# Partial sums copied into the banks of the next products, in a new order of products

## The chip, the cores and the metric

The kernel runs on one core of a Trainium2 chip. The engines of the core work side by side and in order, each on its own list of instructions: TensorE (PE, matmuls, with its weight loads shown apart as PEld), VectorE (DVE), ScalarE (ACT), GpSimd (POOL) and SyncE (SP, which issues most DMAs; ACT issues some). PE writes only into PSUM, here eight banks of 128 x 512 fp32 values. The metric is the device time of one execution in microseconds, the median over several.

## The reference

One layer of a hybrid encoder over 2048 prompt tokens and 64 sample tokens, 1024 wide, in fp32:

```python
mod = (c_act @ w_ada + b_ada)            # six modulation vectors
h = rmsnorm(x, g1) * (1 + sc1) + sh1
u, q, k, v, o, gates = split(h @ w_in)   # pooling mixer and mLSTM side by side
x = x + gt1 * (concat(pool_out, hs) @ w_out)
h2 = rmsnorm(x, g2) * (1 + sc2) + sh2
up = h2 @ w_up                           # 1024 -> 2 x 2816
conv = b_conv + sum(w_conv[j] * upp[:, j:j + T] for j in range(3))   # causal, width 3
a, g = split(conv)
x = x + gt2 * ((silu(g) * a) @ w_down)
y = rmsnorm(x, g_final)
```

It also returns the states that the next call needs (pooling rows, mLSTM matrices, the last two rows of up). The change lies in up = h2 @ w_up and what follows it; some small edits lie in the first stage and in the final norm.

## The kernel before, in words

**Precision.** Each fp32 operand is kept as two parts in PE's reduced fp32 format, hi (a rounded copy, made by ACT) and lo (what is left, made by DVE). A product of two such operands is three passes: hi x hi, hi x lo and lo x hi (PASSES, lines 401 and 1441). Weights come from memory as raw tiles and are split in work_out (L359 on ACT, L362 on DVE). Some splits are kept in memory for later groups (wsplit) and then loaded whole.

**Stages.** Up to about 800 us the kernel does the attention side, in four groups of 512 tokens. Its first stage makes the modulation vectors and the v projection in one (first, L969): for each quarter of the 1024 inputs it builds two slices of h (hi on ACT, lo on DVE) and multiplies them with slices of the weights. From there on it does the feed-forward part, in three groups of 704 tokens (fgroups; g is the group, o the group's record), each in four parts of 5, 5, 6 and 6 pairs (PARTS). A pair f stands for 128 columns of a and the 128 columns of g that gate them. A part first makes its pairs (class Pair, products) and then multiplies them with their rows of w_down for all eight blocks of 128 output columns (down, L1707), adding into x3 (down_end, L1722).

**A pair.** The up-projection uses a Strassen-Winograd scheme with seven half-size products instead of eight: the tokens of the group are two halves of 352, the 1024 inputs two halves of 512. For each pair PE makes seven products, each 12 matmuls of 128 x 352 (L1441), named after their operand on the token side: B11, B21, T2, T3, B22, T1 and T4. Their weights are up_unit 0 (B11), 1 (B21), 3 (T4) and the sums WS2 (T2), WS3 (T3), WS4 (B22) and WS1 (T1), made once by the kernel. Three PSUM banks take them: b1 holds B11, then B11 + T2, then B11 + T2 + T1; b2, which is also b4, holds B21 and then, newly begun, B22; b3 holds T3 and then T3 + T4. The results are

```
a, first half:  B21 + s1     (s1 = B11, copied by ACT, L1480; sum on DVE, L1493)
g, first half:  b3 + u2      (u2 = B11 + T2, L1489; sum_g0, L1449)
a, second half: B22 + u4     (u4 = B11 + T2 + T1, L1504; sum_a, L1449)
g, second half: T3 + u4      (sum_g1, L1449)
```

They are written to ea and eg, from which scale_a and scale_g (ACT, L1424), taps_a and taps_g (DVE, L1429, two each), silu (ACT, L1535), gate (DVE), split_hi (ACT) and split_lo (DVE) make the split operand of the down-projection. The tiles s1, u2, u4 and ea have one buffer each.

**The order.** In the feed-forward stage the order on PE, ACT, DVE and POOL is that in which the Python code calls them (manual_schedule); the order of SP's DMAs is left to a scheduler, apart from DMAs marked keep_in_program_order. The steps of three pairs are interleaved by hand in products: those of this pair, of the one before (old) and of the one before that (older). T4 of the pair before is done by old.last_product, between products of this pair; at the first pair of a part old is None. Weight units are fetched by pump, called ahead of each product, in the order of the list stream: up to seven units ahead, with six tiles for split weights and four for raw ones, and the splits of the next four are issued to ACT and DVE by the same call. Banks come in turn from two pools (mm_ps), six of them here.

**Background work.** Generators in bg are advanced by one step at a time (tick) between products: prepare (norm and token-side operands of the next group, which ACT stores to Bd), reload (which loads them, in the order of BN), final (final norm of the group before, stored by SP, L1606) and final_end (the same for the last group). x3 is loaded from x2d by load_x2 (L1576), two slices per pair.

Of the kernel before, what the change touches and what calls it, by code (L numbers as in the profile page):

```python
# [12 lines left out]
ALU = mybir.AluOpType  # L13
# [32 lines left out]
BN = ("B11", "B21", "T2", "T3", "B22", "T1", "T4")  # L46
# [13 lines left out]
def tile_layer(ctx: ExitStack, tc: tile.TileContext, xT, vecs, cst, rst, rowv, w_mod, w_ada, w_qkou, w_v, w_pool,  # L60
# [242 lines left out]
    for g in range(NFG):  # L303
        for (f0, f1_) in PARTS:
            late = []
            for f in range(f0, f1_):
                stream += [(up_unit(f, 0), 512), (up_unit(f, 1), 512)] + late
                stream += [sum_unit(g, f, i) for i in (WS2, WS3, WS4, WS1)]
                late = [(up_unit(f, 3), 512)]
# [91 lines left out]
    PASSES = ((0, 0), (0, 1), (1, 0))  # L401

# [386 lines left out]
    if True:  # L789
# [128 lines left out]
        def first():  # L918
# [44 lines left out]
            def cells(qn, us):  # L963
                for hv, to in ((1, ps), (0, ps2)):
                    w, n = us[1 - hv].w, VC[hv]
                    for k in (2 * qn, 2 * qn + 1):
                        for ti in range(4):
                            for pi, (a, b) in enumerate(PASSES):
                                pe.matmul(to[ti][:, :n], h[k][:, b, ti * P:(ti + 1) * P],  # L969
                                          w[:, a, k % 2 * n:(k % 2 + 1) * n],  # L970
                                          start=(hv == 1 and k == 0 and pi == 0), stop=(k == KD - 1 and pi == 2),
                                          skip_group_check=hv == 0)
                            yield
# [480 lines left out]
    class Pair:  # L1454
# [9 lines left out]
        def products(self, old):  # L1464
# [15 lines left out]
            act.activation(self.s1, b1[:, :FH], AF.Copy)  # L1480
# [9 lines left out]
            rest((old, Pair.scale_g))  # L1490
            self.ea = ext_tile(o, f, "a")
            for (a, b, d) in spans(o, 0):
                dve.tensor_tensor(out=self.ea[:, d:d + b - a], in0=b2[:, a:b], in1=self.s1[:, a:b], op=ALU.add)  # L1493
            self.b3 = mm_ps()
            product(self.b3, Bo, "T3", True)
            rest((old, Pair.taps_g))
            tick(1)
            product(self.b4, Bo, "B22", True)
            rest((old, Pair.silu))
            product(b1, Bo, "T1", False)  # L1500

        def copy_u4(self):
            self.u4 = half_tile("u4")
            act.activation(self.u4, self.b1[:, :FH], AF.Copy)  # L1504

        def sum_a(self):
            plus(self.o, 1, self.ea, self.u4, self.b4)
# [81 lines left out]
    def final(o, x3, ssum):  # L1589
# [13 lines left out]
        for k in range(KD):  # L1603
            dve.scalar_tensor_tensor(out=x3[k], in0=x3[k], scalar=V[:, V_GF + k:V_GF + k + 1], in1=box[0],
                                     op0=ALU.mult, op1=ALU.mult)
            nc.sync.dma_start(out=yT[k, :, o.t0:o.t0 + FT], in_=x3[k])  # L1606
# [3 lines left out]
    def final_end(o, x3, sums, lo, hi):  # L1610
# [7 lines left out]
        dg = fscr()  # L1618
# [5 lines left out]
        nf, rem = w // P, w % P  # L1624
        blks = [(0, nf, P), (nf, nf + 1, rem)] if rem else [(0, nf, P)]
        for (a, b, n) in blks:
            v = dg[:n, a * P:a * P + (b - a) * n].rearrange("p (t c) -> p t c", c=n)
            dve.tensor_tensor(out=v, in0=ident[:n, :n].unsqueeze(1).broadcast_to([n, b - a, n]),
                              in1=rs[:n, a:b].unsqueeze(2).broadcast_to([n, b - a, n]), op=ALU.mult)
        for _ in range(4 if lo == 0 else 0):  # L1630
            yield
        pb = m2_ps()
        for (a, b, n) in blks:
            c = slice(a * P, a * P + (b - a) * n)
            pe.matmul(pb[:, c], ones[:n, :], dg[:n, c], start=True, stop=True)
# [220 lines left out]
```

## Time and profile before

| | |
|---|---|
| three runs | 2226.63, 2229.96, 2235.10 us; median 2229.96 |
| profiled execution | 2230.7 us; its span 2228.9 us, mean granted PE clock 0.994 |
| PE | busy 2193.3 us, 98% of the span |
| DVE, ACT, POOL | 1573.4, 1004.7 and 197.5 us (71%, 45%, 9%) |
| up-projection matmuls (L1441) | 5544, busy 887.5 us |
| down-projection matmuls (L1707) | 3168, busy 508.2 us |
| DMA | 493.52 MB, mean 221 GB/s |

Times are in microseconds from the span's start unless marked ns. PE's busy time is not time at its peak, since matmuls are pipelined and their ends modelled. A row of the timeline has start, duration, engine, line, operation, out<-in, shape and count, and in brackets the idle time before it with what ended it. A row of the table by line has busy time, mean ns of one, and the idle time before the group with what ended most of it. A row of the table of waits has the waiting engine and line, what it waited for, us in total, times, and the longest. A row of a window has its length, the busy time of PE, PEld, DVE, ACT and POOL with instructions, the granted PE clock, the DMA engines' share and GB/s.

### The profile page before, as it was taken

The page shows a single profiled execution, that of the slowest core. Times are in us where ns is not written, and L with a number is a line of the kernel's source. Part 1 is how long each engine was busy: PE and PEld are TensorE (multiplying, and loading weights), DVE is VectorE, ACT ScalarE, POOL GpSimd, SP SyncE. Part 2 cuts the span into 40 slices and gives each one's busy share as a digit, 9 for nine tenths or more (in the row PEclk, how much of TensorE's full clock was granted, in tenths as well). Part 3 has the DMA queues.
Part 4 walks back from the last instruction along what each step waited for, and adds up shares of the span by engine and source line. Part 5 has one row for each costly group of instructions (what it writes and reads, how often), then busy time and mean ns, then how long its engine had stood idle before and what let it go on. Part 6 is the DMA issues. An engine that isn't in the chain of part 4 may idle for free.

```text
span 2228.9 us, 37979 instructions
## 1 busy us (share of the span) xinstructions
PE 2193.3 (98%) x13720; PEld 2080.2 (93%) x13720; DVE 1573.4 (71%) x2909; ACT 1004.7 (45%) x1992; POOL 197.5 (9%) x475
## 2 busy tenths in 40 slices
PE   7999999999999989999999999999999999999998
PEld 6888888878899989999999999999999999999997
DVE  4878568577856678687868677677757685757474
ACT  3554335234334446464636444445435353445254
POOL 0010001001000100010000110000001210101012
PEclk9999999999999999999999999999999999999999
DMA  9967996997899466657656874556458654353442
GB/s 335 343 237 250 330 313 213 321 314 245 281 309 306 143 234 224 205 180 250 220 160 213 295 251 156 196 191 218 145 170 266 199 196 160 111 179 120 144 152 80
DMA packets 276445, 493.52 MB, mean 221 GB/s; under 512 B 24953, under 2 KB 103417, under 8 KB 276257
## 3 DMA queue, kind: packets, MB, share of 16 engines
q1 hardware_dynamic: 266784, 468.77, 63.1%
q10 hardware_dynamic: 9472, 22.32, 2.6%
q8 instruction: 108, 1.77, 0.3%
q14 instruction: 81, 0.66, 0.1%
HBM read 382.77 MB, written 108.22 MB: 220 GB/s over the span
## 4 chain that ended last, share of the span: by engine, by line
PE 60%; DMA 1%; DVE 1%; issue 0%; ACT 0%; POOL 0%; POOLq 0%; SPq 0%; ACTq 0%; DVEq 0%
PE mm L1441 37%; PE mm L1707 22%; DMA wt<-wsum 1%; DMA yT<-x 0%; ACT tg L1424 0%; DVE tg L1429 0%; DMA wt<-wsplit 0%; DMA x<-x2d 0%; ACT wt L359 0%; PE m L1595 0%; DVE ta L1429 0%; ACT ta L1424 0%; PE m L1621 0%; DVE hx L722 0%; DVE wt L362 0%
## 5 line engine op out<-in xcount | busy, mean ns | idle before, releaser
L1441 PE MATMUL mm<-hx,wt 128*128 128x352 f32 x5544 | 887.5, 321 | 8.8 <-DVE wt L362 5.0
L1441 PEld LDWEIGHTS mm<-hx,wt 128*128 128x128 f32 x5544 | 881.7, 188 | 10.3 <-DVE wt L362 5.2
L1707 PE MATMUL mm<-av,wt 128*128 128x352 f32 (+2 forms) x3168 | 508.2, 321 | 0.0
L1707 PEld LDWEIGHTS mm<-av,wt 128*128 128x128 f32 x3168 | 502.7, 188 | 1.8 <-DVE x L1722 0.4
L415 PE MATMUL mm<-hl,wt 128*128 128x512 f32 (+2 forms) x1920 | 397.4, 359 | 3.7 <-DMA wt<-hl_kept 2.8
L362 DVE TENSOR_TENSOR wt<-raw,wt 128x512 fp32r<-128x512 f32 (+3 forms) x494 | 307.2, 638 | 88.5 <-ACT wt L359 78.7
L415 PEld LDWEIGHTS mm<-hl,wt 128*128 128x128 f32 x1920 | 313.0, 188 | 52.4 <-issue 7.6
L359 ACT ACTIVATE wt<-raw 128x512 fp32r<-128x512 f32 (+3 forms) x494 | 271.2, 570 | 191.3 <-PE mm L1707 81.6
L415 PE MATMUL mm<-mx,wt 128*128 128x512 f32 (+1 forms) x960 | 186.0, 353 | 2.2 <-DVE wt L362 1.6
L1722 DVE SCALAR_TENSOR_TENSOR x<-mm,MOD,x 128x352 f32<-128x352 f32 (+4 forms) x224 | 106.6, 527 | 114.0 <-PE mm L1707 113.9
L415 PEld LDWEIGHTS mm<-mx,wt 128*128 128x128 f32 x960 | 158.7, 188 | 27.6 <-DVE wt L362 1.9
L1429 DVE SCALAR_TENSOR_TENSOR tg<-eg,V,tg 128x704 f32<-128x704 f32 (+1 forms) x132 | 125.7, 952 | 46.9 <-ACT tg L1424 44.4
L362 DVE TENSOR_TENSOR wt<-wt 128x512 fp32r<-128x512 f32 x176 | 121.9, 693 | 45.5 <-ACT wt L359 45.1
L359 ACT ACTIVATE wt<-wt 128x512 fp32r<-128x512 f32 x176 | 110.0, 626 | 69.9 <-DMA wt<-wsum 64.0
L1429 DVE SCALAR_TENSOR_TENSOR ta<-ea,V,ta 128x704 f32<-128x704 f32 (+1 forms) x132 | 125.7, 952 | 8.7 <-ACT ta L1424 6.3
L1564 DVE TENSOR_TENSOR av<-tg,av 128x704 fp32r<-128x704 f32 (+4 forms) x112 | 62.2, 589 | 46.7 <-ACT av L1556 46.4
L1535 ACT ACTIVATE tg<-tg 128x704 f32<-128x704 f32 (+1 forms) x66 | 52.4, 794 | 79.2 <-DVE tg L1429 79.2
L1489 ACT ACTIVATE u<-mm 128x352 f32<-128x352 f32 x66 | 30.6, 464 | 126.5 <-PE mm L1441 90.9
L1449 DVE TENSOR_TENSOR eg<-mm,u 128x352 f32<-128x352 f32 x154 | 70.2, 468 | 22.5 <-ACT u L1504 11.3
L196 DVE SCALAR_TENSOR_TENSOR acc<-raw,CA,acc 128x512 f32<-128x512 f32 x84 | 60.7, 746 | 30.3 <-DMA raw<-w_ada 30.3
L1480 ACT ACTIVATE s<-mm 128x352 f32<-128x352 f32 x66 | 30.6, 463 | 90.0 <-PE mm L1441 89.7
L1037 PE MATMUL mm<-wt,hl 128*128 128x256 f32 (+1 forms) x576 | 70.9, 282 | 0.0
(281 smaller groups left out, 1992.6 us busy)
## 6 DMA issues: line engine op xcount, KB each, us to landing
wt<-hl_kept SPq DMA_DIRECT2D x108, 512.0 KB, 5.7
raw<-w_up SPq DMA_DIRECT2D x198, 256.0 KB, 3.8
wt<-wsum SPq DMA_DIRECT2D x176, 256.0 KB, 4.0
wt<-wsplit SPq DMA_DIRECT2D x88, 512.0 KB, 4.3
raw<-w_down SPq DMA_DIRECT2D x96, 256.0 KB, 2.8
w<-w_up SPq DMA_DIRECT2D x88, 256.0 KB, 5.4
wsum<-w SPq DMA_DIRECT2D x44, 512.0 KB, 4.8
wsplit<-wt SPq DMA_DIRECT2D x44, 512.0 KB, 4.4
```

The costliest lines, as they stand in the source:

```text
L196: dve.scalar_tensor_tensor(out=acc[s], in0=w, scalar=CA[:, k, s:s + 1], in1=acc[s], op0=ALU.mult, op1=ALU.add)
L359: act.activation(u.w[:, 0, :u.n], u.raw[:, :u.n], AF.Copy)
L362: dve.tensor_tensor(out=u.w[:, 1, :u.n], in0=u.raw[:, :u.n], in1=u.w[:, 0, :u.n].bitcast(F32), op=ALU.subtract)
L415: pe.matmul(ps[bi][:, :hi - lo], U[:, a, k % 4 * P:(k % 4 + 1) * P], mv[k][:, b, lo:hi], start=(at == 0 and pi == 0), stop=(k == order[-1] ...
L1037: pe.matmul(ps[ti][:n, :cols], h[4 * kh + k4][:, b, lo:lo + n], U[:, a, k4 % 2 * cols:(k4 % 2 + 1) * cols], start=(kh == 0 and k4 == 0 and ...
L1429: dve.scalar_tensor_tensor(out=t[:, :E], in0=ext[:, j:j + E], scalar=wc(j, f), in1=t[:, :E], op0=ALU.mult, op1=ALU.add)
L1441: pe.matmul(ps[:, :FH], U[:, a, kc * P:(kc + 1) * P], Bo.at(nm, kc, b), start=(first and kc == 0 and pi == 0), stop=(kc == 3 and pi == 2), ...
L1449: dve.tensor_tensor(out=ext[:, d:d + b - a], in0=ps[:, a:b], in1=u[:, a:b], op=ALU.add)
L1535: act.activation(self.tg[:, :E], self.tg[:, :E], AF.Silu)
L1564: dve.tensor_tensor(out=cut(1), in0=self.of_tg(cut(0), a, b), in1=cut(0).bitcast(F32), op=ALU.subtract)
L1707: pe.matmul(ps[i][:, :hi - lo], U[:, a, k % 4 * P:(k % 4 + 1) * P], av[k](b, lo, hi), start=(k == 0 and (a, b) == PASSES[0]), stop=(k == n ...
L1722: dve.scalar_tensor_tensor(out=x3[n][:, a:b], in0=ps[i][:, a - lo:b - lo], scalar=gt2(n, s), in1=x3[n][:, a:b], op0=ALU.mult, op1=ALU.add)
```

## The change

The bank b2 now takes over what ACT and DVE added before. Once B11 is in b1, ACT copies b1 into b2, and B21 accumulates on that; ACT then copies the finished first half of a from b2 to ea (out_a). Once T1 is in b1, ACT copies b1 into b2 again and also to u4, B22 accumulates on the bank, and ACT copies the second half to ea at the start of the next pair (out_a1). The order of products in a pair becomes B11, (T4 of old), T2, B21, T1, T3, B22, and the stream of weights and BN follow it. In the first two pairs of all, one matmul prepares b2 for accumulation. sum_g0 stands ahead of taps_a, and sum_g1 follows T3 in its own pair. The step ahead of the down-projection follows suit.

The other edits: in the first stage the three passes of four matmuls each go in the order hi x hi, then lo weights, then lo of h, four tiles at a time; load_x2 in groups 1 and 2 loads three slices per pair, in program order; the output stores of final go to ACT's queue, one step behind their product; final_end broadcasts the statistics by matmuls with the identity as moving operand, without the DVE product of before, and takes fewer steps.

```diff
-BN = ("B11", "B21", "T2", "T3", "B22", "T1", "T4")
+BN = ("B11", "T2", "B21", "T1", "T3", "B22", "T4")
...
-                stream += [(up_unit(f, 0), 512), (up_unit(f, 1), 512)] + late
-                stream += [sum_unit(g, f, i) for i in (WS2, WS3, WS4, WS1)]
+                stream += [(up_unit(f, 0), 512)] + late + [sum_unit(g, f, WS2), (up_unit(f, 1), 512)]
+                stream += [sum_unit(g, f, i) for i in (WS1, WS3, WS4)]
...
     PASSES = ((0, 0), (0, 1), (1, 0))
+    HIGHS = ((0, 0), (1, 0), (0, 1))
...
-                        for ti in range(4):
-                            for pi, (a, b) in enumerate(PASSES):
-                                pe.matmul(to[ti][:, :n], h[k][:, b, ti * P:(ti + 1) * P],
...
-                            yield
+                        cell = [(pi, a, b, ti) for pi, (a, b) in enumerate(HIGHS) for ti in range(4)]
+                        for i, (pi, a, b, ti) in enumerate(cell):
+                            pe.matmul(to[ti][:, :n], h[k][:, b, ti * P:(ti + 1) * P],
...
+                            if i % 3 == 2:
+                                yield
...
-            rest((old, Pair.copy_u4), (older, Pair.gate))
+            rest((old, Pair.out_a1), (older, Pair.gate))
+            if o.g == 0 and f < 2:
+                pe.matmul(b2[:, :FH], ones_r, Bo.at("B11", 0, 0), start=True, stop=True)
             product(b1, Bo, "B11", True)
-            rest((old, Pair.sum_g1), (old, Pair.sum_a))
-            self.s1 = half_tile("s1")
-            act.activation(self.s1, b1[:, :FH], AF.Copy)
-            rest((older, Pair.split_hi))
-            product(b2, Bo, "B21", True)
-            rest((old, Pair.scale_a), (older, Pair.split_lo))
+            act.activation(b2[:, :FH], b1[:, :FH], AF.Copy)
+            rest((older, Pair.split_hi), (old, Pair.scale_a), (older, Pair.split_lo))
             if old:
                 old.last_product()
-            rest((old, Pair.taps_a), (old, Pair.sum_g0))
+            rest((old, Pair.sum_g0), (old, Pair.taps_a))
             product(b1, Bo, "T2", False)
             self.u2 = half_tile("u2")
             act.activation(self.u2, b1[:, :FH], AF.Copy)
             rest((old, Pair.scale_g))
+            product(b2, Bo, "B21", False)
             self.ea = ext_tile(o, f, "a")
-            for (a, b, d) in spans(o, 0):
-                dve.tensor_tensor(out=self.ea[:, d:d + b - a], in0=b2[:, a:b], in1=self.s1[:, a:b], op=ALU.add)
+            self.out_a(0)
+            product(b1, Bo, "T1", False)
+            act.activation(b2[:, :FH], b1[:, :FH], AF.Copy)
+            self.u4 = half_tile("u4")
+            act.activation(self.u4, b1[:, :FH], AF.Copy)
+            rest((old, Pair.taps_g))
             self.b3 = mm_ps()
             product(self.b3, Bo, "T3", True)
-            rest((old, Pair.taps_g))
             tick(1)
-            product(self.b4, Bo, "B22", True)
+            self.sum_g1()
             rest((old, Pair.silu))
-            product(b1, Bo, "T1", False)
-
-        def copy_u4(self):
...
-        def sum_a(self):
-            plus(self.o, 1, self.ea, self.u4, self.b4)
+            product(self.b4, Bo, "B22", False)
+
+        def out_a(self, half):
+            for (a, b, d) in spans(self.o, half):
+                act.activation(self.ea[:, d:d + b - a], self.b4[:, a:b], AF.Copy)
+
+        def out_a1(self):
+            self.out_a(1)
...
-            nc.sync.dma_start(out=x, in_=x2d[k, :, o.t0:o.t0 + FT])
+            got = nc.sync.dma_start(out=x, in_=x2d[k, :, o.t0:o.t0 + FT])
+            if o.g > 0:
+                tc.keep_in_program_order(got)
...
-            nc.sync.dma_start(out=yT[k, :, o.t0:o.t0 + FT], in_=x3[k])
+            yield
+            act.dma_start(out=yT[k, :, o.t0:o.t0 + FT], in_=x3[k])
...
-            v = dg[:n, a * P:a * P + (b - a) * n].rearrange("p (t c) -> p t c", c=n)
-            dve.tensor_tensor(out=v, in0=ident[:n, :n].unsqueeze(1).broadcast_to([n, b - a, n]),
-                              in1=rs[:n, a:b].unsqueeze(2).broadcast_to([n, b - a, n]), op=ALU.mult)
-        for _ in range(4 if lo == 0 else 0):
+        for _ in range(3 if lo == 0 else 0):
             yield
...
-            pe.matmul(pb[:, c], ones[:n, :], dg[:n, c], start=True, stop=True)
+        for ti, (t, n) in enumerate(tiles):
+            pe.matmul(pb[:, t - lo:t - lo + n], rs[:n, ti:ti + 1].broadcast_to([n, P]), ident[:n, :n],
+                      start=True, stop=True)
...
                     if lo == 0:
                         yield
-                        yield
...
-                    x3 += load_x2(o, range(len(x3), min(len(x3) + 2, KD)))
+                    x3 += load_x2(o, range(len(x3), min(len(x3) + (3 if o.g else 2), KD)))
...
-            pair.copy_u4()
-            todo.extend([both_of(pair.sum_g1, old.gate), both_of(pair.sum_a, old.split_hi), both_of(old.split_lo, pair.scale_a)])
+            pair.out_a1()
+            todo.extend([old.gate, old.split_hi, both_of(old.split_lo, pair.scale_a)])
```

More of the change, by code (lines that the diff above doesn't have):

```diff
@@ L966, in cells @@
                     for k in (2 * qn, 2 * qn + 1):
-                        for ti in range(4):
-                            for pi, (a, b) in enumerate(PASSES):
[L969 to L972, printed above, removed]
-                            yield
+                        cell = [(pi, a, b, ti) for pi, (a, b) in enumerate(HIGHS) for ti in range(4)]
+                        for i, (pi, a, b, ti) in enumerate(cell):
+                            pe.matmul(to[ti][:, :n], h[k][:, b, ti * P:(ti + 1) * P],
+                                      w[:, a, k % 2 * n:(k % 2 + 1) * n],
+                                      start=(hv == 1 and k == 0 and pi == 0), stop=(k == KD - 1 and pi == 2),
+                                      skip_group_check=hv == 0)
+                            if i % 3 == 2:
+                                yield
             for qn in range(4):
@@ L1617, in final_end @@
         rs = f1.tile([P, 5], F32, tag="rs", name="rs", bufs=2)
-        dg = fscr()
         for ti, (t, n) in enumerate(tiles):
```

7 lines of the change are left out of this document (removed).

## The prediction

> **What bounds the kernel now.** I read the page's busy times and chain first, then who TensorE (PE) waited for, then the timeline at the places that the change touches, then the rows by shape.
>
> ```profile
> span 2228.9 us, 37979 instructions
> PE 2193.3 (98%) x13720; PEld 2080.2 (93%) x13720; DVE 1573.4 (71%) x2909; ACT 1004.7 (45%) x1992; POOL 197.5 (9%) x475
> L1441 PE MATMUL mm<-hx,wt 128*128 128x352 f32 x5544 | 887.5, 321 | 8.8 <-DVE wt L362 5.0
> ...
> PE mm L1441 <- DVE wt L362: 5.0, 1, 5.0
> PE mm L969 <- DVE hl L913: 2.8, 4, 0.8
> PE mm L1441 <- ACT wt L359: 2.0, 2, 1.4
> PE mm L1441 <- DVE ea L1493: 1.8, 2, 1.3
> ```
>
> PE is idle for 2228.9 - 2193.3 = 35.6 us in all. In the up-projection (L1441), where most of the edit lies, it is idle for 8.8 us out of some 900, and five waits make up all of that. So work taken from VectorE (DVE) is not by itself time taken from the end: only PE's idle time can be won, and every new wait of PE is paid in full.
>
> **The change, part by part.** The profiled execution took 2230.7 us (1.8 around its span); the median of the runs is 2229.96, 0.7 lower. The sum is made against 2230.7.
>
> *Copies instead of sums.* Each of the 66 pairs loses two or three DVE sums into ea and a ScalarE (ACT) copy s, and gains two ACT copies from a bank into a bank and two or three from a bank into ea.
>
> ```profile
> L1480 ACT ACTIVATE s<-mm 128x352 f32<-128x352 f32 x66 | 30.6, 463 | 90.0 <-PE mm L1441 89.7
> L1493 DVE TENSOR_TENSOR ea<-mm,s 128x352 f32<-128x352 f32 x66 | 34.2, 519 | 1.1 <-PE mm L1441 1.0
> L1449 DVE TENSOR_TENSOR ea<-mm,u 128x352 f32<-128x352 f32 x44 | 22.7, 517 | 0.0
> ...
> 1636.70:1690.00 53.30, 53.30 (x338) 53.30 (x338) 40.19 (x60) 28.22 (x48) 3.91 (x16) 1.00 0.54 177
> ```
>
> The last row is four steady pairs (PE, PEld, DVE, ACT, POOL busy): PE is never idle, DVE has 40.2 and ACT 28.2 of 53.3 us. DVE loses 4 x 2 x 0.52 = 4.2 there and ACT gains 4 x 3 x 0.46 = 5.6, both under a full PE: worth nothing at the end and costing nothing, as long as no copy is late. The cover is what changes. Before, T2, which adds onto the bank that s is read from, came two products after B11. Now one product (T4 of the pair before) stands between, and B22, which adds onto the bank that the second copy fills, has one (T3). A product takes 12 x 0.158 = 1.9 us (53.30 / 338), and a copy needs 0.46: some 1.2 us to spare.
>
> *The first pair of each part.* Here old is None, so no T4 stands between: B11, copy, T2. Twelve times (3 groups x 4 parts) PE must wait. The timeline where the last part of group 1 begins, and the one place where T2 waited for s:
>
> ```profile
> 1625.29 9.03 PE L1441 MATMUL mm<-hx,wt 128*128 128x352 f32 x56
> 1627.39 0.47 ACT L1480 ACTIVATE s<-mm 128x352 f32<-128x352 f32 x1 [5.78 <-PE mm L1441]
> ...
> 1499.27 4.94 PE L1441 MATMUL mm<-hx,wt 128*128 128x352 f32 x29
> 1501.14 0.50 ACT L715 ACTIVATE fscr<-fscr 128x352 fp32r<-128x352 f32 x1 [2.27 <-DMA Bd<-fscr]
> 1502.64 0.44 ACT L1480 ACTIVATE s<-mm 128x352 f32<-128x352 f32 x1
> 1503.13 0.95 PEld L1441 LDWEIGHTS mm<-hx,wt 128*128 128x128 f32 x6 [0.18 <-ACT s L1480]
> ```
>
> The product after B11 would start at 1625.29 + 12 x 0.158 = 1627.19; the copy ends at 1627.86, and PE's weight load follows an end by 0.05 (1503.13 after 1502.64 + 0.44). That is 0.72 us, and a restart costs 0.09 more: in the row 1787.87 below, 7 matmuls after a wait take 1.36 us where 0.32 + 6 x 0.158 = 1.27 would do. 12 x 0.81 = 9.7 us. Bounds: the row has SBUF as its target, and no row shows ACT writing a bank; with no copy time at all 12 x 0.35 = 4.2, with the copy's time doubled, for a bank at both ends (0.93 us), 15.3. I take the row itself, the nearest. The Trainium skill (ScalarE: Activation LUTs, Step-by-step: what each stage is for) says that ScalarE writes PSUM faster than SBUF, and its page Perfetto Trace Analysis (Optimizing Scalar/DVE Operations) gives access overheads of about 51 ns against 93 ns. No run here shows it; by these figures the copy would be 0.42 us, an estimate, and the term 9.2 us.
>
> At one of the twelve (1499.27) ACT was late: B11 ended near 1501.33 and its copy began at 1502.64, behind splits that waited for a store. Between them two products hid it; now it is paid: 1.3 us (0 to 1.3). Another cost follows some waits: a slower pace.
>
> ```profile
> 1503.50:1510.50 7.00, 7.00 (x44) 7.00 (x43) 1.00 0.83 297
> ...
> 1511.50:1518.50 7.00, 7.00 (x47) 7.00 (x46) 1.00 0.88 270
> ```
>
> Behind the wait at 1503.13 PE began 44 matmuls in 7 us at a clock of 1.00, later 47: 3 x 0.158 = 0.47 us lost. The rows 1787.87 and 1322.46 below show no such stretch (22 matmuls in 3.74 us). With 12 new waits that is 0 to 5.6 us; I take a third, 1.8.
>
> *Late weights at the second part's start.* PE already waits in the first pair of two parts:
>
> ```profile
> 934.36 1.27 ACT L359 ACTIVATE wt<-wt 128x512 fp32r<-128x512 f32 x2 [4.47 <-DMA wt<-wsum]
> 936.30 1.90 PE L1441 MATMUL mm<-hx,wt 128*128 128x352 f32 x10 [1.29 <-DVE ea L1493]
> 1401.88 1.40 PE L1441 MATMUL mm<-hx,wt 128*128 128x352 f32 x7 [0.51 <-DVE ea L1493]
> ```
>
> A landing time doesn't move because PE lost 0.81 us three products earlier, so 0.81 + 0.51 = 1.3 us of the new waits are not paid twice. The new stream asks for WS2 and WS1 earlier and WS3 and WS4 later, on the same slots and in the same sum; I cost it at nothing (+-1.0).
>
> *The output stores and the order sums.* In the third pair of groups 1 and 2 PE waits for weight splits; the chain runs back through u, which waits for the DVE sum behind both taps, to a weight load that SyncE (SP) issued behind an output store.
>
> ```profile
> 1309.29 0.31 SPq L1606
> 1309.70 6.72 DMA wt<-wsum
> ...
> 1322.46 3.74 PE L1441 MATMUL mm<-hx,wt 128*128 128x352 f32 x22 [1.37 <-ACT wt L359]
> 1787.87 1.36 PE L1441 MATMUL mm<-hx,wt 128*128 128x352 f32 x7 [0.63 <-ACT wt L359]
> ```
>
> The 16 stores go to ACT's queue, one step after their product; the x2d loads no longer stand between the stores but behind them, pinned; and sum_g0 stands ahead of taps_a, so that u is free before the taps and not behind them. Won: 1.37 + 0.63 = 2.0. Lost: each store now stands in ACT's order and waits there for a DVE product, and a copy may stand behind it; with 1.2 us to spare I take 0.2. Net 1.8 (0 to 2.0). The loads that now come late (three, then five) stand before the down-projection, which needs them one at a time: nothing.
>
> *The first stage.* In L969 each quarter waits for the low half of h, made by DVE; the new order puts eight matmuls ahead of its first use.
>
> ```profile
> 22.15 3.45 PE L969 MATMUL mm<-wt,hl 128*128 128x264 f32 x14 [0.80 <-DVE hl L913]
> 34.17 1.97 PE L969 MATMUL mm<-wt,hl 128*128 128x264 f32 x14 [0.68 <-DVE hl L913]
> 0.00:60.00 60.00, 48.70 (x492) 38.87 (x493) 27.92 (x62) 21.05 (x40) 3.52 (x17) 0.91 0.95 333
> ```
>
> 14 matmuls take 1.97, so eight cover 1.1 us: all four waits (2.8 us by the table) go. The DMA engines are 0.95 busy, so some may come back as a wait for weights: I take 2.4 (0 to 2.8).
>
> *The end.* The DVE product L1628 goes; two small matmuls make the broadcast directly, and the first block's outputs need fewer steps, so that four of them no longer stand before the statistics.
>
> ```profile
> 2218.43 2.21 DVE L1658 TENSOR_TENSOR y<-x,m 128x448 f32<-128x448 f32 x4
> 2219.49 0.36 PE L1621 MATMUL m<-ones_r,fscr 128*128 128x1 f32 x2
> 2220.55 0.16 DVE L1585 TENSOR_SCALAR rs<-m 128x2 f32<-128x2 f32 x1
> 2221.53 0.42 DVE L1628 TENSOR_TENSOR fscr<-ident,rs 128x256 f32<-128x256 f32 x1 [0.82 <-POOL rs L1587]
> ```
>
> From 2219.85 to 2220.55 the statistics stood behind them (0.6), and L1628 with its hand-over is 0.5, less 0.1 for more matmuls: 1.0 (0.4 to 1.2). The two matmuls that prepare the banks once cost 0.3.
>
> **Sum.** 9.7 + 1.3 + 1.8 - 1.3 + 0.3 = 11.8 lost; 1.8 + 2.4 + 1.0 = 5.2 won; +6.6. 2230.7 + 6.6 = 2237.3, or 2236.6 from the median: I say 2236.5.
>
> **The rivals.**
> *ScalarE's queue is late for the copies in steady pairs.* For it: ACT sits in order behind weight splits.
>
> ```profile
> ACT wt L359 <- DMA wt<-wsum: 64.0, 52, 4.5
> ACT u L1489 <- DVE wt L362: 30.3, 14, 2.6
> ACT u L1489 <- PE mm L1441: 90.9, 42, 4.2
> ```
>
> If 14 waits like those of u (2.2 us each) fell ahead of a copy, each would cost 2.2 - 1.2 = 1.0: 14 us, 2251. It decides from 1.2 us of lateness on. Against it: the four steady pairs above have ACT idle for nearly half, and 42 of the 66 u copies waited for PE last.
>
> *DVE's relief clears the stall where the up-projection begins* (the other side: not slower). PE waits there 4.98 us for a DVE weight split, and comes back at half its clock:
>
> ```profile
> 818.93 6.30 PE L1441 MATMUL mm<-hx,wt 128*128 128x352 f32 x25 [4.98 <-DVE wt L362]
> 819.00:823.00 4.00, 4.00 (x14) 4.00 (x15) 2.35 (x4) 0.73 (x2) 0.00 (x0) 0.50 0.76 261
> 936.30:940.00 3.70, 3.70 (x22) 3.70 (x23) 2.35 (x4) 1.36 (x3) 0.00 (x0) 1.00 0.58 178
> ```
>
> Half clock: 14 matmuls in 4.0 us instead of 25, 1.7 us. All of it gone is 6.7: 2237.3 - 6.7 = 2230.6, no change. For it: another order of the first weights there. Against it: the sums that go stand behind this stall, not ahead of it.
>
> *Short waits lower PE's clock.* Were each of the 12 waits followed by such a stretch, 12 x 1.7 = 20 us: 2257. Against it: behind the wait of 1.29 us the clock stayed at 1.00 (last row). The Trainium skill (TensorE: Matmul & The Clock Gate, A second HAM failure mode: psum-queue depth-cycling) says that frequent short idles between groups that cycle through banks make the clock swing; another section there (HAM oscillation — how this bites in real kernels) sets the danger at gaps above 3.4 us. The two rows agree with the latter, and by it this rival gives nothing.
>
> **How the numbers follow.** Forecast 0.60 (own range 2230 to 2243, by the bounds above taken half way), late copies 0.18, stall cleared 0.17, clock 0.05. About 0.5% (11 us, 2218.8 to 2241.1) is what a measurement tells from no change. Slower: 0.17 + 0.05 and 0.10 from the forecast's upper end, 0.32; faster: 0.05, where the stall clears and the copies cost their lower bound; same 0.63. Range 2226 to 2251.
>
> **What would show it.** Right: twelve waits of T2 of about 0.8 us on the copy at the parts' starts and none in other pairs; no wait of L969 on hl; no output store on SP's queue; DVE down by some 70 us, ACT up by some 95, PE's busy time unchanged. Wrong: waits of T2 or B22 in many pairs (late copies), the wait near 819 gone, or a granted clock below 1.00 behind the parts' starts.

## The result, and the profile after

| | before | after |
|---|---|---|
| median | 2229.68 us (2226.63 to 2235.10, 8 runs) | 2237.88 us (2233.47 to 2244.14, 8 runs) |
| profiled execution, span | 2230.7, 2228.9 us | 2236.88, 2235.1 us |

The ratio is 1.0042 (95% interval 1.0030 to 1.0055): 9.4 us slower by the ratio (the two medians are 8.2 apart), beyond the prediction's 0.5% only at the interval's upper end. In the two profiled executions it is 6.2 us.

From the page of after, then its table by line and by shape, then its table of waits:

```profile
span 2235.1 us, 38015 instructions
PE 2200.0 (98%) x13728; PEld 2084.2 (93%) x13728; DVE 1508.7 (68%) x2752; ACT 1078.4 (48%) x2212; POOL 198.3 (9%) x475
```
```profile
L1443 PE MATMUL mm<-hx,wt 128*128 128x352 f32 x5544 | 892.8, 322 | 12.6 <-ACT mm L1482 10.2 <-DVE wt L362 2.2 <-ACT u L1489 0.2
...
L1495 ACT ACTIVATE mm<-mm 128x352 f32<-128x352 f32 x66 | 29.6, 448 | 49.8 <-PE mm L1443 49.1 <-DVE wt L362 0.7
L1482 ACT ACTIVATE mm<-mm 128x352 f32<-128x352 f32 x66 | 29.6, 448 | 66.7 <-PE mm L1443 66.5
```
```profile
PE mm L1443 <- ACT mm L1482: 10.2, 12, 3.0
...
PE mm L1443 <- DVE wt L362: 2.2, 1, 2.2
...
PE mm L1706 <- ACT av L1560: 1.1, 2, 0.6
```

VectorE is 64.7 us less busy and ScalarE 73.7 us more. The up-projection (now L1443) waits twelve times for the copy into b2 (L1482), 10.2 us in all; the waits on ea and on ScalarE's weight splits, 3.8 us before, are gone from it. L1706 is the down-projection. PE's idle time hardly moved (35.1 us, 35.6 before), while its busy time rose by 6.7 us. Half clock (a granted clock of 0.50, at which a matmul takes twice as long and counts as busy) isn't the reason in sum: the mean granted clock is 0.994 in both profiles. Part of every wait counts as busy too: of some 0.8 us that a short one costs below, 0.54 show as idle time.

Idle time therefore doesn't add up to the difference. Milestones do: the start of the first matmul of each stretch, in after less in before. The up-projection begins at 796.33 us instead of 803.15, so after is 6.8 us ahead there, and the run ends some 6 us behind. By stretch, in us, from one profile of each kernel (a minus is a gain; "third pairs" are the first parts of groups 1 and 2, "late ScalarE" the third parts of groups 0 and 1; the columns after the first are kernels of the experiments below):

| stretch | after | up-projection alone | x2d loads undone | loads and stores undone | T3 ahead of T2 | and B22 anew, late x2d loads | the same in all 12 parts |
|---|---|---|---|---|---|---|---|
| up to the up-projection | -6.8 | -3.8 | -3.4 | -4.8 | -4.5 | -3.4 | -3.4 |
| very first part | +1.8 | -0.2 | -0.9 | +2.8 | +1.6 | +1.4 | -2.6 |
| second parts, groups 0 and 1 | -0.9 | +0.2 | -0.9 | -0.9 | +5.1 | -1.0 | 0.0 |
| third pairs | -0.9 | -0.8 | +6.1 | -0.8 | 0.0 | -2.5 | -2.5 |
| late ScalarE | +6.3 | +7.4 | +6.2 | +6.4 | +2.4 | +0.3 | -0.5 |
| other five parts | +4.2 | +4.8 | +4.6 | +4.8 | +4.3 | 0.0 | 0.0 |
| down-projection behind the third-pair parts | +3.2 | 0.0 | 0.0 | 0.0 | +5.8 | +0.1 | +0.1 |
| other down-projections, and the end | -0.7 | +0.2 | -0.8 | -0.3 | -0.3 | -0.4 | -0.6 |

Among kernels with the same code there, the first two rows vary by up to 4 us from one execution to the next. Most others repeat to some tenths where the construction is the same, so that one profile tells more of them than medians do. The profile with T3 ahead of T2 is the longest of its runs (2245.2 us, median 2240.8), which shows in its second parts.

**Two first pairs.** The timeline of after, first at the third part of group 1, then at the last part of group 2, which is a plain one (its copy starts as soon as B11 is done):

```profile
1499.84 0.50 ACT L716 ACTIVATE fscr<-fscr 128x352 fp32r<-128x352 f32 x1 [4.53 <-DMA Bd<-fscr]
...
1501.55 0.45 ACT L1482 ACTIVATE mm<-mm 128x352 f32<-128x352 f32 x1
...
1502.04 5.13 PE L1443 MATMUL mm<-hx,wt 128*128 128x352 f32 x22 [3.03 <-ACT mm L1482]
...
2094.01 2.07 PE L1443 MATMUL mm<-hx,wt 128*128 128x352 f32 x12
2096.11 0.45 ACT L1482 ACTIVATE mm<-mm 128x352 f32<-128x352 f32 x1 [3.17 <-PE mm L1443]
2096.47 0.62 ACT L359 ACTIVATE wt<-wt 128x512 fp32r<-128x512 f32 x1
2096.62 1.54 PE L1443 MATMUL mm<-hx,wt 128*128 128x352 f32 x8 [0.54 <-ACT mm L1482]
```

In the plain one T2 starts 2.61 us after B11 instead of 12 x 0.158 = 1.90: 0.71 lost, and 0.11 more in the first step after it, which takes 0.27 by the trace. In the other, ScalarE stood 4.53 us behind a store of prepare, and PE waited 3.03 us. What followed is in the last two of these windows; the ones above are of the first stage (columns as before):

```profile
0.00:60.00 60.00, 52.84 (x519) 43.34 (x520) 29.25 (x64) 25.23 (x45) 3.52 (x17) 0.94 0.99 351
...
20.30:27.90 7.60, 7.57 (x92) 6.40 (x93) 3.69 (x7) 1.81 (x3) 0.00 (x0) 0.78 1.05 385
27.90:36.40 8.50, 8.50 (x115) 7.31 (x114) 4.61 (x10) 2.56 (x4) 0.00 (x0) 1.00 1.06 389
...
1502.00:1505.50 3.50, 3.46 (x13) 3.46 (x14) 1.60 (x4) 0.53 (x1) 0.00 (x0) 0.56 0.63 228
1505.50:1509.00 3.50, 3.50 (x24) 3.50 (x23) 1.09 (x2) 1.97 (x4) 0.00 (x0) 1.00 0.02 5
```

Behind the long wait PE ran 3.5 us at a clock of 0.56 and began 13 matmuls instead of 22, some 1.4 us lost. The same two quarters of the first stage, before:

```profile
20.90:30.70 9.80, 8.94 (x91) 6.91 (x92) 3.72 (x7) 1.83 (x4) 0.00 (x0) 0.65 1.05 386
30.70:40.10 9.40, 8.72 (x116) 7.39 (x115) 4.61 (x10) 2.44 (x4) 0.00 (x0) 1.00 1.05 392
```

The first quarter is 2.2 us shorter and the second 0.9.

**The x2d loads.** The timeline of after ahead of the down-projection, first part of group 1:

```profile
1349.03 2.32 SPq L1580 DMA_DIRECT2D x<-x2d  x5
...
1351.45 11.41 SPq L343 DMA_DIRECT2D raw<-w_down  x5
...
1357.28 0.31 ACT L359 ACTIVATE wt<-raw 128x128 fp32r<-128x128 f32 x1 [3.65 <-DMA raw<-w_down]
1357.50 0.96 ACT L1426 ACTIVATE tg<-eg,V 128x704 f32<-128x704 f32 x1
...
1363.13 0.59 PE L1706 MATMUL mm<-av,wt 128*128 128x352 f32 x2 [0.62 <-ACT av L1560]
```

Five x2d loads stand on SP ahead of the last weights for w_down. ScalarE waits 3.65 us for such a weight, scale_g (L1426) of the part's last pair stands behind it, and the down-projection has to wait for that pair's operand av. The granted clock is 1.00 throughout these waits (1360 to 1372 us), so the 1.3 us of half clock that an expectation below puts here aren't in the trace: what is lost is idle time, and a slower step after each of two stops.

### The profile page after: what moved, and what is told of

Its sections match the earlier page's. It is cut to its first block, busy times and chain, and to the rows that moved or that the text cites. A ratio compares the mean times of both kernels' runs of the same rounds, so it can differ in the third digit from the quotient of the medians.

```text
span 2235.1 us, 38015 instructions
## 1 busy us (share of the span) xinstructions
PE 2200.0 (98%) x13728; PEld 2084.2 (93%) x13728; DVE 1508.7 (68%) x2752; ACT 1078.4 (48%) x2212; POOL 198.3 (9%) x475
## 5 line engine op out<-in xcount | busy, mean ns | idle before, releaser
L1443 PE MATMUL mm<-hx,wt 128*128 128x352 f32 x5544 | 892.8, 322 | 12.6 <-ACT mm L1482 10.2
L1443 PEld LDWEIGHTS mm<-hx,wt 128*128 128x128 f32 x5544 | 883.9, 188 | 17.0 <-ACT mm L1482 13.8
L1706 PE MATMUL mm<-av,wt 128*128 128x352 f32 (+2 forms) x3168 | 509.4, 321 | 1.5 <-ACT av L1560 1.1
L1706 PEld LDWEIGHTS mm<-av,wt 128*128 128x128 f32 x3168 | 502.7, 188 | 4.6 <-ACT av L1560 2.0
L359 ACT ACTIVATE wt<-raw 128x512 fp32r<-128x512 f32 (+3 forms) x494 | 279.1, 574 | 204.2 <-PE mm L1706 109.3
L1508 ACT ACTIVATE ea<-mm 128x352 f32<-128x352 f32 (+1 forms) x154 | 62.6, 421 | 112.4 <-PE mm L1443 109.0
L1039 PEld LDWEIGHTS mm<-wt,hl 128*128 128x128 f32 x576 | 69.3, 188 | 1.0 <-issue 0.6
```

The lines of the kernel that those rows point to most:

```text
L359: act.activation(u.w[:, 0, :u.n], u.raw[:, :u.n], AF.Copy)
L1039: pe.matmul(ps[ti][:n, :cols], h[4 * kh + k4][:, b, lo:lo + n], U[:, a, k4 % 2 * cols:(k4 % 2 + 1) * cols], start=(kh == 0 and k4 == 0 and ...
L1443: pe.matmul(ps[:, :FH], U[:, a, kc * P:(kc + 1) * P], Bo.at(nm, kc, b), start=(first and kc == 0 and pi == 0), stop=(kc == 3 and pi == 2), ...
L1508: act.activation(self.ea[:, d:d + b - a], self.b4[:, a:b], AF.Copy)
L1706: pe.matmul(ps[i][:, :hi - lo], U[:, a, k % 4 * P:(k % 4 + 1) * P], av[k](b, lo, hi), start=(k == 0 and (a, b) == PASSES[0]), stop=(k == n ...
```

## The experiments

Ratios are to before, run beside each kernel, with 95% intervals. The first theory was the prediction's: every uncovered copy is paid in full, and the other edits win some of it back. The milestones had added a cost of the x2d loads and a larger gain in the first stage.

**The other edits alone.** The up-projection, its stream and the steps ahead of the down-projection are those of before; all else as in after.

> The other edits alone: the up-projection, its weight stream and the steps ahead of the down-projection are those of before; the first stage, the x2d loads, the output stores and the end are those of after. By the prediction's terms: 2.4 (first stage) + 1.0 (end) + up to 1.8 (third pairs; the order of the sums, which is part of that, is not in this kernel) = 3.4 to 5.2 won, a ratio of 0.9977 to 0.9985. By the traces of before and after, where the up-projection begins 6.8 us earlier: 6.8 + 0.4, less what the pinned x2d loads cost at the down-projections of the first parts of groups 1 and 2 (waits on av, 1.8 + 1.4): 4 us, 0.998. What tells them apart is the trace: if the pinned loads make those waits, they stand here too (L1706 on av, some 1.3 us in all); if the new order of steps in the pair makes them, they do not.

Measured 0.9988 (0.9979 to 0.9997). The waits on av are smaller (0.5 us in all), but the two down-projections lose 2.3 us by the milestones: the loads cost there with the old order of steps too. The waits for weight splits in the same parts only move, from the third pairs to the fourth (1.6 us, 2.0 before): the stores on ScalarE's queue and the pinned loads don't cure these.

**The up-projection alone**, on before.

> The up-projection alone, on before: ACT's copies into the banks, the new order of products, the weight stream and the steps ahead of the down-projection; nothing else. The prediction's terms: 9.7 + 1.3 + 1.8 - 1.3 + 0.3 = 11.8 lost, of which up to 2.0 may be won back in the third pairs by the new order of the sums: a ratio of 1.0044 to 1.0053, with twelve waits of T2 on the copy, ten of them 0.8 us. Rival (the loss of after comes from the x2d loads and the stores on ACT's queue, and the waits are hidden by what follows): 1.002 or less. If the pinned x2d loads make the waits of the down-projection on av, none stands here.

Measured 1.0054 (1.0037 to 1.0071). From the table of waits:

```profile
PE mm L1441 <- ACT mm L1480: 11.0, 12, 3.5
```

With the other edits alone it adds up to after: +0.0054 - 0.0012 = +0.0042. No wait on av, and none in the third pairs. The prediction's 11.8 us for this part are 0.0053.

**The first stage alone**, on before: the order hi x hi, lo weights, lo of h.

```diff
+    HIGHS = ((0, 0), (1, 0), (0, 1))
...
-                            for pi, (a, b) in enumerate(PASSES):
+                        cell = [(pi, a, b, ti) for pi, (a, b) in enumerate(HIGHS) for ti in range(4)]
```

> The order of the three passes in the first stage alone, on before. The prediction's term: 2.4 won (2.8 by the table of waits, less what comes back), 0.9988. By the milestones of after (the first stage ends 5.1 us earlier): 5.1 less 0.8 that stands ahead of the edit and is a matter of the first load: 4.3, 0.9981. The trace separates them: the four waits of 0.7 to 0.8 us go in both; in the second each quarter is 0.85 us shorter and the first gains 1.3 more, because the stretch of the first six quarter matmuls runs without a break.

Measured 0.9978 (0.9968 to 0.9988), 4.9 us: nearer the second expectation, and the first lies at the interval's end. By the medians this one edit wins more than all the side edits together, and the remaining ones (loads, stores, end) cost about 0.001 between them; the intervals alone don't show that difference, but 2.3 us of loss are there in the down-projections above.

**The x2d loads undone**, in after.

```diff
-            if o.g > 0:
-                tc.keep_in_program_order(got)
...
-                    x3 += load_x2(o, range(len(x3), min(len(x3) + (3 if o.g else 2), KD)))
+                    x3 += load_x2(o, range(len(x3), min(len(x3) + 2, KD)))
```

> The kernel after, but the x2d loads as in before: two slices per pair, placed by the scheduler and not pinned. Theory (five pinned loads stand on SP's queue ahead of the last weights for w_down, whose split stands ahead of scale_g on ACT): the waits of the down-projection on av in the first parts of groups 1 and 2 go, with their half clock: 2 to 3.2 won against after, a ratio to before of 1.0028 to 1.0033. Rival (the steps in their new order are late by themselves): 1.0042, the waits stay. Second rival (the loads go back between the stores and the weights, and the third pairs wait for weights again as in before, 1.37 + 0.63): 1.0038 to 1.0045, with waits of L1443 on weight splits.

Measured 1.0055 (1.0041 to 1.0069). The waits on av go, as the theory had it, and 6.1 us are lost in the parts of the third pairs (at two third pairs and a fifth, 3.41 us at half clock behind the longest wait included): the second rival, at three times the price. From the tables of waits of this kernel, PE's and SP's:

```profile
PE mm L1443 <- ACT mm L1495: 4.2, 3, 2.2
...
SPq L1580 <- DMA yT<-x: 31.9, 11, 7.1
```

The x2d loads wait in SP's queue for the stores that free their tiles, weight loads stand behind them, a weight split on ScalarE stands behind those, and the copy for B22 behind the split. Before, only a weight was late; now the copy is late with it.

**Loads and stores undone**, both as in before, in after.

```diff
-            yield
-            act.dma_start(out=yT[k, :, o.t0:o.t0 + FT], in_=x3[k])
+            nc.sync.dma_start(out=yT[k, :, o.t0:o.t0 + FT], in_=x3[k])
```

> The kernel after, but x2d loads and output stores both as in before (the stores on SP's queue). Theory (third pairs wait because an x2d load that waits for its store stands in SP's queue ahead of a weight load; with both on SP the scheduler places them so that the weights come in time, as in the up-projection alone, whose third pairs did not wait): no wait of B22 at the third pairs (4.2 us in the kernel with the loads alone undone), no wait of the down-projection on av; the sum of the up-projection alone (1.0054) and the first stage alone (0.9978): 1.0032. Rival (the stores were not the cause, the new order in the pair makes third pairs late with any placement of the loads): 1.005 or more, waits on the copy at third pairs.

Measured 1.0024 (1.0014 to 1.0035; the sum of the two parts, 1.0032, lies inside), with no wait worth naming in third pairs and none on av. With stores and loads both on SP the loads wait far less, from the same view:

```profile
SPq L1580 <- DMA yT<-x: 8.1, 6, 2.5
```

So moving the stores brings the stall back in the third pairs, pinning the loads takes it out again at the price of the down-projections, and leaving both alone has neither.

**The copy twice.** In each first pair ScalarE makes the copy two times.

```diff
-            act.activation(b2[:, :FH], b1[:, :FH], AF.Copy)
+            for _ in range(1 if old else 2):
+                act.activation(b2[:, :FH], b1[:, :FH], AF.Copy)
```

> The kernel after, but in the first pair of each part ACT makes the copy from b1 into b2 twice, one behind the other. Theory (what PE waits for is paid one to one): each of twelve waits grows by the copy's 0.45 us, 5.4 in all, with no more half clock except at the longest: 1.0042 + 0.0024 = 1.0066; the ten waits of 0.70 become 1.15. Rival (a longer wait is hidden by what follows, late weights for one): 1.0042 to 1.005. Rival (waits above one us bring half clock with them, 1.2 to 2 us each): 14 to 24 us more, 1.012 or above.

Measured 1.0065 (1.0052 to 1.0078): 0.0023 more, 5.1 us of the 5.4 expected. From its table of waits:

```profile
PE mm L1443 <- ACT mm L1483: 15.8, 12, 3.3
```

5.6 us more in twelve waits. The plain ones are 1.18 us instead of 0.70, none of them followed by half clock.

**T3 ahead of T2** in eleven first pairs (all but the very first), as cover for the copy; in these pairs it no longer stands behind T1.

```diff
             if old:
                 old.last_product()
+            early = old is None and (o.g or f)
+            if early:
+                self.b3 = mm_ps()
+                product(self.b3, Bo, "T3", True)
```

> The kernel after, but in the first pair of eleven of the twelve parts T3 stands between B11 and T2 (the weight stream follows; the very first part is left as it is). Theory (the uncovered copy is the loss): a product of 1.9 us covers the copy, eleven waits of T2 go. In the trace of after they are 9 x 0.81 + 2.07 + 3.5 = 12.9 us, and some 1.2 of half clock behind the longest; 1.3 may come back as the late weights that before had in two of these pairs, and 1.5 of the longest stays: 9 to 13 won against after, a ratio to before of 0.9985 to 1.0003. Rival (WS3, fetched two units earlier, makes T3 or T2 wait for weights instead): 0.5 to 1.3 us at most parts, 1.002 to 1.004. Rival (waits as short as 0.8 us cost nothing in the end): 1.004, no change.

Measured 1.0039 (1.0025 to 1.0053): next to nothing won, and by none of the three reasons. From its table of waits and its timeline:

```profile
PE mm L1445 <- ACT mm L1501: 7.3, 11, 0.9
...
PE mm L1445 <- ACT mm L1484: 1.2, 2, 0.7
```
```profile
1985.32 0.45 ACT L1501 ACTIVATE mm<-mm 128x352 f32<-128x352 f32 x1 [0.92 <-PE mm L1445]
...
1985.82 2.49 PE L1445 MATMUL mm<-hx,wt 128*128 128x352 f32 x14 [0.60 <-ACT mm L1501]
```

T2's wait (L1484) is gone and eleven waits on the second copy (L1501) stand in its place: T3 had been the cover between T1 and B22. I had looked at one copy of the pair only. Where ScalarE is late T3 does help: 2.4 us are lost there instead of 6.3.

**The same, with late x2d loads.** Only the slices of the first three output blocks are loaded ahead of the down-projection.

```diff
-                x3 += load_x2(o, range(len(x3), KD))
+                x3 += load_x2(o, range(len(x3), NE))
...
                 down(pss[n], Ws[n], [nf - 2], both)
+            x3 += load_x2(o, range(len(x3), KD))
```

> As the kernel with T3 ahead of T2, and of the x2d loads only those of the first three output blocks stand ahead of the down-projection in groups 1 and 2; the other five follow its first two thirds. Theory (these five loads on SP's queue hold up the last weights for w_down, whose split stands ahead of scale_g on ACT): the two waits of the down-projection on av (1.28 and 0.68 us in after, with 1.3 us of half clock) go, 2 to 3 us less than with T3 alone. Rival (the chain is late by itself): the waits stay, no difference. Rival (loads that come later hold up down_end, which adds into them): waits of the matmuls on banks, slower than with T3 alone by 1 to 4 us.

Measured 1.0016 (1.0005 to 1.0027), and no wait on av: the five loads were the cause.

**T3 ahead of T2, and B22 begun anew** in those pairs (its sum with u4 on VectorE, as before), so that neither copy is uncovered.

```diff
-            act.activation(b2[:, :FH], b1[:, :FH], AF.Copy)
+            self.fresh = early
+            if not early:
+                act.activation(b2[:, :FH], b1[:, :FH], AF.Copy)
...
-            product(self.b4, Bo, "B22", False)
+            product(self.b4, Bo, "B22", self.fresh)
...
         def out_a1(self):
-            self.out_a(1)
+            if self.fresh:
+                plus(self.o, 1, self.ea, self.u4, self.b4)
+            else:
+                self.out_a(1)
```

> As the kernel with T3 ahead of T2 in eleven first pairs, and in those pairs B22 begins its bank anew, with the sum of u4 on DVE as before, so that the second copy, which had lost its cover T3, is not needed. Theory (each uncovered copy is paid one to one, and moving T3 only moved the wait to B22): the waits of 0.76 us at B22 go as well, 11 x 0.87 = 9.6 won against the kernel with T3 alone (1.0039): 0.9996; the x2d loads still cost their waits on av. Rival (PE waits at these places for something else too, weights or banks): waits of 0.5 us or more stay in first pairs, 1.002 to 1.004.

Measured 1.0002 (0.9991 to 1.0012), 0.0037 less than with T3 alone, where the theory had 0.0043. The other five parts lose 0.0 us.

**Both at once.**

> Both at once: no uncovered copy in eleven first pairs, and five of the x2d loads behind the first part of the down-projection. By the theories: 1.0016 (T3 with the later loads) less 11 x 0.87 = 9.6 us (0.0043): 0.9973, 2225 us, faster than both kernels. Then what is left against before is the first stage's gain alone (0.9978 by itself), and accumulating on copied banks gains nothing by itself. Rival (as above): 0.999 to 1.0016.

Measured 0.9979 (0.9967 to 0.9991): 4.7 us faster than before. That is what the first stage wins by itself. So with its waits taken away, no gain or loss of accumulating on copied banks shows beyond the intervals, about 0.1% on either side.

**The same in all twelve parts**, the very first included.

> The kernel of 0.9979 (no uncovered copy in eleven first pairs, late x2d loads), with the twelfth first pair, the very first, done in the same way. There T2 waits 0.87 us while PE runs at half clock. Theory: that wait goes, 0.9 us, 0.9975, which the interval does not tell from 0.9979; the trace does. Rival (the weights WS3 and the operand T3, asked for earlier at the place where weights are short, lengthen the wait ahead of it by 1 to 3 us): 0.998 to 0.999, and a longer wait on a weight split near 815.

Measured 0.9947 (0.9934 to 0.9961), 2221.16 us beside 2231.76 for before: the fastest of all, and more than either expectation. Windows of the kernel with eleven parts, then of this one:

```profile
810.00:820.00 10.00, 5.63 (x20) 4.94 (x19) 6.58 (x13) 2.86 (x6) 0.00 (x0) 0.64 0.51 182
820.00:826.00 6.00, 6.00 (x33) 5.97 (x33) 0.53 (x3) 1.97 (x4) 0.29 (x1) 0.75 0.67 243
```
```profile
810.00:820.00 10.00, 7.95 (x43) 7.72 (x41) 5.62 (x11) 2.42 (x5) 0.00 (x0) 0.83 0.68 222
820.00:826.00 6.00, 6.00 (x41) 5.97 (x41) 2.15 (x6) 2.72 (x6) 2.82 (x4) 1.00 0.69 227
```

In the first, the wait for weights is followed by T2's wait for the copy, and PE is still below full clock after 820. In the second there is one stretch of half clock. The very first part is 4.0 us shorter: 1.8 us are the first wait itself (2.0 us here, 3.8 there), some 0.8 T2's wait, and the rest goes with the shorter half clock (3.4 us in all, 10.2 there). Whether the first wait is shorter by the edit or by chance stays open, and so do the 3 us by which the two ratios (five runs in this one) differ more than the profiles.

**First stage, end, and the order of the sums** (sum_g0 ahead of taps_a), on before.

> Before, with three of the side edits only: the first stage's order, the end, and sum_g0 ahead of taps_a (no copy into a bank, no new order of products, stores and x2d loads as before). Theory (the third pairs of groups 1 and 2 wait because u comes late behind the taps, and the order of the two sums alone cures it): their two waits of 1.4 and 0.6 us on weight splits go; with the first stage's 0.9978 and some 0.4 us at the end: 0.9967. Rival (in the kernel with the up-projection alone they went for another reason, the new stream or the new order of products): the waits stay, 0.9976.

Measured 0.9989 (0.9979 to 0.9999), no better than the first stage alone (0.9978, the intervals overlap). The third pairs wait 2.4 and 1.5 us instead of 1.4 and 0.6, now for the sum into ea. In the old order of products the order of the sums is no cure; in the kernel with the up-projection alone the third pairs went with it and the new order of products together.

## Why the prediction was right, and where its terms were not

The forecast of 2236.5 us lies 1.4 below the median of 2237.88, and the mechanism was the one named: new waits of PE at twelve places, partly paid back by side edits. Several terms were wrong, and cancelled; that the sum comes so close is luck.

- **The first pairs, 9.7 us.** Right. Ten waits of T2 lose 0.71 + 0.11 = 0.82 us each (0.81 forecast), and the copy twice shows that they are paid one to one. The bound from the copy into SBUF held: 0.45 us into a bank against 0.46. The Trainium skill (ScalarE: Activation LUTs, Step-by-step: what each stage is for) has PSUM as the faster target; the trace agrees in sign (448 against 463 ns), by a third of the 0.04 us of the estimate, which rests on the Trainium skill's page Perfetto Trace Analysis (Optimizing Scalar/DVE Operations).
- **ScalarE late, 1.3 us.** The step that failed most on the side of losses. It took the lateness at one place from before, as if it stayed the same. In after there are two such places (third parts of groups 0 and 1): T2 starts 1.96 and 3.20 us late there (1.79 and 3.03 of it idle time), two restarts cost 0.2, and half clock behind the longer wait costs 1.4, less 0.5 of slower pace that before had at this place. The two parts lose 6.3 us; the forecast's share for them was 2 x 0.81 + 1.3 = 2.9.
- **Slower pace, 1.8 us.** Too much: matmuls of the up-projection that start 0.163 to 0.2 us behind the one before cost 0.9 us before and 1.3 after (over 0.158 each), and in after half of them lie from 852 to 864 us, behind no wait of T2. What came instead is the half clock above.
- **Late weights, -1.3.** Right, and more: the two second parts are together 0.9 us shorter although each has its wait of 0.82, and show no wait for weights.
- **The third pairs, -1.8 with the stores, loads and sums.** The waits went as forecast, the reason given was not it: neither the stores and loads alone nor the order of the sums on the old products takes them away. And "The loads that now come late (three, then five) stand before the down-projection, which needs them one at a time: nothing" is wrong: it costs 3.2 us. I had asked who needs the loads, and not what stands behind them on SP's queue.
- **The first stage, -2.4.** Mis-sized: 4.9 us by itself. Its waits (2.8) all went, and 60 us into the run after is 5.2 us ahead. I reckoned with weights coming late instead, since the DMA engines were 0.95 busy; they became 0.99 busy, and nothing waited. The clock is only part of the rest (0.78 instead of 0.65 in the first quarter of these two profiles). Where the granted clock stays at 1.00 through the stage, it takes 35.0 us from its first matmul to its last with the old order (the up-projection alone, 2.8 us idle) and 31.5 with the new one (the other edits alone): 3.5 us, since a wait costs more than its idle time. Before and after take 37.6 and 32.7; the half clock in them, more in before, differs from execution to execution.
- **The end, -1.0.** 0.4 by the milestones of after, 0.0 in the mean of the eleven kernels that have the edit, 0.4 and 0.5 lost in the two that lack it: worth some 0.3, less than the lower bound of 0.4 and inside the spread of the eleven (0.5 won to 0.6 lost).
- **The signs.** Twelve waits of T2, ten of them plain, and none in steady pairs; no wait of the first stage on the low half of h; VectorE down by 65 (70 forecast), ScalarE up by 74 (95). PE's busy time was to stay and rose by 6.7 us: 4.0 in the very first part, 0.8 in each of the two down-projections, 1.1 in the third part of group 1 with its half clock, some 0.3 at most other new waits, and 1.6 less ahead of the up-projection. One sign of being wrong came true at one of the twelve places: the clock of 0.56 behind the long wait.
- **The rivals.** Late copies in steady pairs: none in after; the kernel with the loads alone undone shows that this needs only a queue in front, three waits of up to 2.2 us. The stall where the up-projection begins: shorter, not gone (2.2 us, and then T2's wait at half clock); the part as a whole lost 1.8. The clock: plain waits of 0.70 and 1.18 us brought no half clock. With the Trainium skill's rule (TensorE: Matmul & The Clock Gate, HAM oscillation — how this bites in real kernels: the danger begins at gaps above 3.4 us) the short waits agree; the long one doesn't, since 3.03 us of idle time were enough.

## What to carry to other kernels

Count the products between a copy and its reader at the ends of the loop too, and for every copy of the iteration: moving one cover uncovered the other. For each DMA that is pinned or moved, ask who is next in that queue, and who stands on his engine behind the one who waits for it. When idle time doesn't explain a difference, compare milestones by stage: here they showed costs and gains of 1 to 7 us under a total of 6.

## What was not expected of the hardware

- The granted clock was either 1.00 or 0.50. In all fourteen profiles half clock came in stretches of 3.41 us, or of two or three times that, which all start on one grid of 3.41 us through the run (only the last stretch is cut off by the end). What goes with it is the idle time of PE inside one piece of this grid. Outside the first 30 us and the end, behind a piece at full clock, the next piece was at half clock in all 31 cases of 1.88 us of idle time or more, in five of the eight between 1.72 and 1.84, and in none below 1.65.
- So the length of a wait alone doesn't decide. In the up-projection outside the very first part, idle times of 2.85 to 3.49 us were always followed by half clock, of seven between 2.19 and 2.41 three were, and of the shorter ones none; in the down-projection one of 1.68 us was. Here are two of 2.37 us each, the first (loads and stores undone) mostly inside one piece, the second (the copy twice) in two:

```profile
1501.23:1504.64 3.41, 1.30 (x8) 1.30 (x9) 2.46 (x5) 2.31 (x5) 0.00 (x0) 1.00 0.81 285
1504.64:1508.05 3.41, 3.41 (x13) 3.41 (x12) 0.94 (x2) 0.98 (x2) 0.00 (x0) 0.50 0.55 181
```
```profile
1503.82:1507.23 3.41, 2.08 (x14) 1.79 (x12) 0.70 (x2) 1.36 (x3) 0.00 (x0) 1.00 0.96 363
1507.23:1510.64 3.41, 2.37 (x14) 2.37 (x15) 2.11 (x4) 1.56 (x5) 0.00 (x0) 1.00 0.80 250
1510.64:1514.06 3.42, 3.42 (x23) 3.42 (x22) 1.11 (x2) 1.90 (x4) 0.00 (x0) 1.00 0.15 56
```

- A second short wait (T2's, 0.54 us idle, 1.02 with the copy twice) within some 5 us of the first goes with longer half clock. Behind a first wait of 2.0 to 3.2 us in the very first pair, half clock lasts 3.41 us in the four kernels without the second wait, and 6.83 in four of the five with it.
- PE waits some 450 us into the run for a load from hl_kept (2.8 us before, 1.6 in after, 1.3 to 3.1 in the others), in code that no edit touches. This, the stall where the up-projection begins (2.0 to 5.0 us) and the half clock in the first 30 us (none to 10.2 us) make up much of the spread between executions of one kernel as far as the profiles show it.
